# A hybrid decoder layer on one core: the loads and adaLN matmuls of the head in another order

## The chip, the cores and the metric

The kernel runs on one NeuronCore of a Trainium2 chip. The metric is device microseconds of one execution. A profiled execution gives a trace of the engines: PE (TensorE, with its weight loads as PEld), DVE (VectorE), ACT (ScalarE), POOL (GpSimd), and SP, which here only issues DMAs.

## What is computed

One decoder layer (depth 1) over 320 tokens: 256 of a prompt and 64 of eight samples with eight tokens each. Nine conditioning vectors (one for the prompt, eight for the samples) give shifts, scales and gates (adaLN); all tokens share the weights. D is 2048, the FFN is 5632 wide, there are four heads, everything is float32. Cut to what matters here:

```python
mod = silu(c) @ w_ada + b_ada                      # w_ada is 2048 x 12288
sh1, sc1, g1, sh2, sc2, g2 = split(mod, 6)
h = rmsnorm(x, norm1_g) * (1 + sc1) + sh1
q, k, v, og, u, ga, gb, alr = split(h @ w_in)      # 11280 columns
loga = log_sigmoid(alr @ w_a2 + b_a) / 16
o, s_new = gla(q, k, v, loga, s0)                  # gated linear attention
y_a = rmsnorm(o) * silu(og)
y_b = pool(u)                                      # causal averages, then w_pool
x = x + g1 * ((sigmoid(ga) * y_a + sigmoid(gb) * y_b) @ w_o)
h2 = rmsnorm(x, norm2_g) * (1 + sc2) + sh2
x = x + g2 * ((silu(gate(h2)) * up(h2)) @ w_down)  # then a final rmsnorm
```

The outputs are y for both groups, the new attention states and the new pooling buffers.

## The kernel before

Activations are kept transposed: 16 k tiles of 128 channels by 320 tokens. Each is split into a high part and a rest in the fast float32 form (`hilo`, lines 315 and 316: `hh` on ACT, `hl` on DVE), and so is each weight tile (`split`, lines 151 and 152: `whi` on ACT, `wlo` on DVE). A product is three matmuls, `whi`·`hh`, `whi`·`hl` and `wlo`·`hh` (`mm3`, lines 165 to 167). Weights come by `raw_chunk` (line 143) on SP's queue, at most 512 KB a load, into three buffers.

**The head** is the block under `with tc.tile_pool(name="head")`. It makes the modulation of the first norm and the projections of group 0 (a group is a head h with its share of q, k, u, v, og, ga, gb: 2816 columns). Since the first projection needs a k tile of h, which needs two blocks of 128 columns of w_ada's sections 0 (shift) and 1 (scale), the k tiles are taken in four slices, `SLICES = ((0, 2), (2, 4), (4, 8), (8, 16))`. A slice runs seven units over its k tiles: q, k, u with 256 columns (`proj`) and v, og, ga, gb with 512 (`proj2`). Their sums are added up over the slices in SBUF (`evac`, line 369). While one slice is projected, the list `bg` makes the next slice's k tiles: for every two blocks `hada(0, b, nb)`, `hada(1, b, nb)` and `h_unit(b, nb)`, spread evenly behind the seven units.

`ada` (before only) takes two blocks of one section. It loads four tiles of 512 KB (four k tiles by 256 columns); each tile gives four matmuls with the 32-column stationary `scT[:, k]` (silu of the conditioning vectors), one on each of the four column groups of PE, where column group j sums every fourth k (line 225). A copy (line 228), two transposes (`tr`, line 129) and a reduction over the four groups (line 233) follow, then bias, +1 and norm gain (lines 236 to 240). The ring has seven tiles.

`h_unit` makes a k tile: three transposes of x, a copy to `xT` (line 461), which is written to a DRAM scratch `xspill` from POOL's queue (line 463; it is read back in the output projection), a product with the norm factors `rx` (line 462), the modulation `affine` (lines 320 to 322) and `hilo`. `rx` comes from sums of squares on ACT (line 443).

The low-rank gate projection `alr_proj` uses all 16 k tiles; it stands behind unit k of the last slice and ends with the tile `alr` (line 484). Its weights `walr` (16 columns of w_in), the masks and constants are loaded on POOL's queue; the program has them in the last slice, but nothing holds them there.

**After the head** its pool is closed, and pools for group 0's recurrence and for the rest of adaLN open in the same memory (memsets at line 534 on). Group 0's recurrence and pooling steps (`queue`, taken by `pump`) run between the projections of groups 1 to 3. Those groups have 11 units each over all 16 k tiles, and the rest of w_ada is done in `ada_burst`: four k tiles by eight blocks at a time, where column group j has its own two blocks, and the sum over k is made in PSUM (line 284). q, k, v and u have one buffer each, so group 1's q can be written (line 371) only when group 0's steps have read theirs (line 622 last), and the products of a unit have two PSUM buffers (`pmain`). The output projection and the FFN follow.

The order on each engine is made by a list scheduler: it walks a simulated time line and takes, of what is ready, what stands first in the program. `tc.high_priority()` moves instructions ahead of that, and `tc.issue_after(i)` holds a block's instructions behind instruction i of the same engine.

Of the kernel before, what the change touches and what calls it, by code (L numbers as in the profile page):

```python
# [38 lines left out]
SLICES = ((0, 2), (2, 4), (4, 8), (8, 16))  # L39

# [42 lines left out]
def body(tc, A):  # L83
# [130 lines left out]
    def ada(sec, b0, nb=2, pool=None, bufs=2):  # L214

        pool = pool or apool[0]
        blk = sec * KT + b0
        w = nb * P
        ps = misc()
        step = 8 // nb  # L220
        for k0 in range(0, KT, step):
            raw = raw_chunk(wada[:, k0:k0 + step, blk * P:(blk + nb) * P], step, w, pool, "araw", bufs)
            for i in range(step):
                j, r = (k0 + i) % 4, (k0 + i) // 4
                PE.matmul(ps[32 * j:32 * j + 32, 0:w], lhsT=scT[:, k0 + i, :], rhs=raw[:, i, :],
                          start=r == 0, stop=r == 3, tile_position=(0, 32 * j))
        sb = pool.tile([P, w], F32, tag="adasb", name=nm("adasb"))
        S.copy(sb, ps[:, 0:w])
        pt = misc()
        for i in range(nb):  # L230
            tr(pt[:, i * P:(i + 1) * P], sb[:, i * P:(i + 1) * P])
        dst = mod[:, blk:blk + nb, :]
        V.tensor_reduce(dst, pt[:, 0:w].rearrange("p (b j r) -> p b r j", b=nb, j=4)[:, :, 0:9, :],
                        axis=AX.X, op=ALU.add)
        bb = bada[:, blk:blk + nb].unsqueeze(2).broadcast_to([P, nb, 9])
        V.tensor_tensor(dst, dst, bb, op=ALU.add)
        if sec in (1, 4):
            g = N1G if sec == 1 else N2G
            V.tensor_scalar(dst, dst, 1.0, None, op0=ALU.add)
            V.tensor_tensor(dst, dst, g[:, b0:b0 + nb].unsqueeze(2).broadcast_to([P, nb, 9]), op=ALU.mult)  # L240

# [155 lines left out]
    with tc.tile_pool(name="head", bufs=1) as xp:  # L397
        junk = xp.tile([P, D], F32, name="junk")
        crow = junk[0:9, :]
# [3 lines left out]
        G.memset(xn[2][TS:P], 0.0)  # L403
        x2d = A["x_prompt"][0]
        V.memset(scT, 0.0)
        make_identity(nc, ident)
        pt = misc()
        for k in range(KT):
            tr(pt[:, 16 * k:16 * k + 9], crow[:, k * P:(k + 1) * P])
        csig = xp.tile([P, KT, 9], F32, name="csig")  # L410
        crT = pt[:, 0:256].rearrange("p (k r) -> p k r", r=16)[:, :, 0:9]
        S.activation(csig, crT, AF.Sigmoid)
        V.tensor_tensor(scT[:, :, 0:9], crT, csig, op=ALU.mult)
# [4 lines left out]
        nc.sync.dma_start(vr0, A["b_ada"].rearrange("o (r p) -> (o r) p", p=P))  # L418
        vr1 = xp.tile([4 * KT + 4, P], F32, name="vr1")
        for j, n in enumerate(("norm1_g", "norm2_g", "final_norm_g", "pool_scale")):  # L420
            a = A[n] if n == "final_norm_g" else A[n][0]
            nc.sync.dma_start(vr1[16 * j:16 * j + 16, :], a.rearrange("(r p) -> r p", p=P))
        nc.sync.dma_start(vr1[64:68, :], A["gla_norm_g"][0].rearrange("(r p) -> r p", p=P))

        def hada(sec, b, nb):
            ada(sec, b, nb, *head_ring)

        head_ring = [xp, 7]

        pt = misc()  # L430
# [4 lines left out]
        V.tensor_scalar(bada[:, 4 * KT:5 * KT], bada[:, 4 * KT:5 * KT], 1.0, None, op0=ALU.add)  # L435
        hada(0, 0, SLICES[0][1])
        hada(1, 0, SLICES[0][1])

        ssq = xp.tile([P, 3], F32, name="ssq")
        V.memset(ssq, 1.0)  # L440
        for i in range(3):
            n = P if i < 2 else TS
            S.activation(junk[:n], xn[i][:n], AF.Square, accum_out=ssq[:n, i:i + 1])
        S.activation(ssq, ssq, AF.Sqrt, scale=1.0 / D, bias=epst)
        V.reciprocal(ssq, ssq)
        prs = misc()
        dg = xp.tile([P, 3, P], F32, name="dg")
        for i in range(3):
            V.tensor_scalar(dg[:, i], ident, ssq[:, i:i + 1], None, op0=ALU.mult)
            PE.matmul(prs[:, i * P:(i + 1) * P], lhsT=ones, rhs=dg[:, i], start=True, stop=True)  # L450
        rx = xp.tile([P, T], F32, name="rx")
        V.tensor_copy(rx, prs[:, 0:T])

        def h_unit(k0, nk):
            for k in range(k0, k0 + nk):
                pt = misc()
                for i in range(3):
                    tr(pt[:, i * P:(i + 1) * P], xn[i][:, k * P:(k + 1) * P])
                xT = xp.tile([P, T], F32, tag="xT", bufs=2, name=nm("xT"))
                xh = xp.tile([P, T], F32, tag="xh", bufs=2, name=nm("xh"))  # L460
                S.copy(xT, pt[:, 0:T])
                V.tensor_tensor(xh, pt[:, 0:T], rx, op=ALU.mult)
                nc.gpsimd.dma_start(xspill[k], xT)
                affine(xh, 1, 0, k)
                hilo(hh[k], hl[k], xh)
# [23 lines left out]
        new_gates(g0)  # L489
        for si, (k0, k1) in enumerate(SLICES):  # L490
            if si == 0:
                h_unit(0, SLICES[0][1])
            bg = []
            if si + 1 < len(SLICES):
                n0, n1 = SLICES[si + 1]
                st_ = min(2, n1 - n0)
                for b in range(n0, n1, st_):
                    nb = st_
                    bg += [lambda b=b, nb=nb: hada(0, b, nb), lambda b=b, nb=nb: hada(1, b, nb),
                           lambda b=b, nb=nb: h_unit(b, nb)]  # L500
            elif si == len(SLICES) - 1:
                walr = xp.tile([P, KT, 16], F32, name="walr")
                nc.gpsimd.dma_start(walr, win[:, :, OAL:OAL + 16])
                nc.gpsimd.dma_start(msk, A["ci"])
                cum = xp.tile([P, NM0 + NM1 + NMS], F32, name="cum")
                nc.gpsimd.dma_start(cum, A["cf"][:, CFC:CFW])
                nc.gpsimd.dma_start(cst[:, 2 * P:], A["cf"][:, 0:CFC])
            us = units(0)
            us = [u for u in us if u[0] in "qku"] + [u for u in us if u[0] not in "qku" and u[1] == 0]
            done = 0  # L510
            for ui, (kind, i, col) in enumerate(us):
# [5 lines left out]
                if si == len(SLICES) - 1 and ui == 1:  # L517
                    alr_proj(walr, cum)
                want = len(bg) * (ui + 1) // len(us)
                while done < want:  # L520
                    bg[done]()
                    done += 1
# [376 lines left out]
    def pump(n):  # L899
        for _ in range(min(n, len(queue))):  # L900
            queue.pop(0)()

    nc.gpsimd.dma_start(A["o_ps"][0, :, 0:PB - LS, :], A["state_pool"][0, :, LS:PB, :])

    st, E = gla_steps(g0)
    pst, psy = pool_steps(g0)
# [289 lines left out]
```

## Time and profile before

| | |
|---|---|
| median of 3 runs | 1974.52 us (1974.08 to 1975.68) |
| the profiled execution | 1972.61 us, of which the trace spans 1970.7 us |
| PE, DVE, ACT, POOL busy | 1927.2, 1003.3, 822.3, 204.7 us |
| w_ada loads on SP's queue | 64 of 512 KB |
| w_in loads on SP's queue | 173 |
| HBM read / written | 374.23 / 24.67 MB |
| first projection matmul | 38.40 us |

A row of a group of instructions has line, engine, operation, output and inputs, shapes and count, then the busy time in us and the mean duration in ns, then the idle time of the engine ahead of them and what ended most of it. Matmuls overlap in the trace: a projection matmul lasts some 310 ns in its row, but the next one starts well before that ends, so the distance between starts is what it costs. A row of the time line has the start, the length, the engine, the line and the operation; several alike are merged with their count.

### The profile page before, as it was taken

The page shows a single profiled execution, that of the slowest core. Times are in us where ns is not written, and L with a number is a line of the kernel's source. Part 1 is how long each engine was busy: PE and PEld are TensorE (multiplying, and loading weights), DVE is VectorE, ACT ScalarE, POOL GpSimd, SP SyncE. Part 2 cuts the span into 40 slices and gives each one's busy share as a digit, 9 for nine tenths or more (in the row PEclk, how much of TensorE's full clock was granted, in tenths as well). Part 3 has the DMA queues.
Part 4 walks back from the last instruction along what each step waited for, and adds up shares of the span by engine and source line. Part 5 has one row for each costly group of instructions (what it writes and reads, how often), then busy time and mean ns, then how long its engine had stood idle before and what let it go on. Part 6 is the DMA issues. An engine that isn't in the chain of part 4 may idle for free.

```text
span 1970.7 us, 34879 instructions
## 1 busy us (share of the span) xinstructions
PE 1927.2 (98%) x13900; PEld 1811.9 (92%) x13900; DVE 1003.3 (51%) x1894; ACT 822.3 (42%) x1472; POOL 204.7 (10%) x352
## 2 busy tenths in 40 slices
PE   5999999999999999999999999999999999999998
PEld 3778988988899889988989999999999999999998
DVE  2655655655356535665474444444444444444554
ACT  3323553643345433553344333433333434344444
POOL 1002211221122112111130000000000000000000
PEclk9999999999999999999999999999999999999999
DMA  9995558758865787479935554444444444444443
GB/s 339 340 338 181 189 174 292 246 192 312 279 218 168 267 292 261 129 254 326 320 114 194 191 184 142 149 153 144 157 146 152 149 152 150 150 148 149 140 150 107
DMA packets 310206, 400.95 MB, mean 203 GB/s; under 512 B 12898, under 2 KB 273858, under 8 KB 309706
## 3 DMA queue, kind: packets, MB, share of 16 engines
q1 hardware_dynamic: 279914, 291.17, 45.8%
q0 software_dynamic: 30128, 107.55, 14.8%
q8 instruction: 109, 1.79, 0.4%
q14 instruction: 55, 0.44, 0.1%
HBM read 374.23 MB, written 24.67 MB: 202 GB/s over the span
## 4 chain that ended last, share of the span: by engine, by line
PE 82%; DMA 2%; ACT 1%; DVE 1%; issue 0%; POOL 0%; ACTq 0%; DVEq 0%; POOLq 0%
PE ps L167 25%; PE ps L165 25%; PE ps L166 25%; PE pm L284 3%; PE pm L129 1%; DMA araw<-w_ada 1%; PE pm L779 1%; PE pm L758 1%; DMA raw<-w_o 1%; PE pm L723 1%; DMA raw<-w_in 1%; PE pm L712 0%; DVE wlo L152 0%; PE pm L653 0%; ACT whi L151 0%
## 5 line engine op out<-in xcount | busy, mean ns | idle before, releaser
L152 DVE TENSOR_TENSOR wlo<-raw,whi 128x512 fp32r<-128x512 f32 x941 | 648.9, 694 | 773.6 <-ACT whi L151 760.7
L151 ACT CAST whi<-raw 128x512 fp32r<-128x512 f32 x941 | 579.2, 621 | 899.9 <-PE ps L166 802.2
L165 PE MATMUL ps<-hh,whi 128*128 128x320 f32 x1408 | 441.8, 314 | 3.1 <-ACT whi L151 2.1
L167 PE MATMUL ps<-hh,wlo 128*128 128x320 f32 x1408 | 436.0, 312 | 2.0 <-DVE wlo L152 1.9
L166 PE MATMUL ps<-hl,whi 128*128 128x320 f32 x1408 | 436.4, 310 | 0.0
L165 PE MATMUL ps<-h2h,whi 128*128 128x320 f32 x1408 | 434.6, 309 | 0.0
L166 PE MATMUL ps<-h2l,whi 128*128 128x320 f32 x1408 | 434.3, 309 | 0.0
L167 PE MATMUL ps<-h2h,wlo 128*128 128x320 f32 x1408 | 434.2, 309 | 0.0
L165 PEld LDWEIGHTS ps<-hh,whi 128*128 128x128 f32 x1408 | 264.5, 188 | 27.6 <-issue 16.1
L167 PEld LDWEIGHTS ps<-hh,wlo 128*128 128x128 f32 x1408 | 263.7, 188 | 17.5 <-issue 9.5
L166 PEld LDWEIGHTS ps<-hl,whi 128*128 128x128 f32 x1408 | 264.7, 188 | 4.3 <-issue 3.2
L165 PEld LDWEIGHTS ps<-h2h,whi 128*128 128x128 f32 x1408 | 264.5, 188 | 1.2 <-ACT ah L315 1.2
L166 PEld LDWEIGHTS ps<-h2l,whi 128*128 128x128 f32 x1408 | 264.5, 188 | 0.0
L167 PEld LDWEIGHTS ps<-h2h,wlo 128*128 128x128 f32 x1408 | 264.5, 188 | 0.0
L166 PE MATMUL ps<-al,whi 128*128 128x320 f32 (+1 forms) x668 | 206.3, 309 | 0.0
L167 PE MATMUL ps<-ah,wlo 128*128 128x320 f32 (+1 forms) x668 | 205.7, 308 | 0.0
L165 PE MATMUL ps<-ah,whi 128*128 128x320 f32 (+1 forms) x668 | 205.7, 308 | 0.0
L166 PEld LDWEIGHTS ps<-al,whi 128*128 128x128 f32 x668 | 125.2, 187 | 0.1
L167 PEld LDWEIGHTS ps<-ah,wlo 128*128 128x128 f32 x668 | 125.2, 187 | 0.0
L165 PEld LDWEIGHTS ps<-ah,whi 128*128 128x128 f32 x668 | 125.2, 187 | 0.0
L165 PE MATMUL ps<-mh,whi 128*128 128x320 f32 x256 | 80.3, 314 | 3.3 <-ACT whi L151 2.6
L260 POOL DMA_DIRECT2D araw<-w_ada x64 | 45.7, 718 | 355.6 <-PE pm L284 341.0
(316 smaller groups left out, 1698.5 us busy)
## 6 DMA issues: line engine op xcount, KB each, us to landing
raw<-w_gu SPq DMA_DIRECT2D x176, 512.0 KB, 3.4
raw<-w_in SPq DMA_DIRECT2D x173, 512.0 KB, 3.9
araw<-w_ada POOLq DMA_DIRECT2D x64, 1024.0 KB, 8.0
raw<-w_down SPq DMA_DIRECT2D x80, 512.0 KB, 3.4
raw<-w_ada SPq DMA_DIRECT2D x64, 512.0 KB, 6.3
S<-state_gla POOLq DMA_DIRECT2D x16, 1024.0 KB, 8.8
o_gs<-S POOLq DMA_DIRECT2D x16, 1024.0 KB, 6.1
raw<-w_o SPq DMA_DIRECT2D x32, 512.0 KB, 7.3
```

What stands on the lines that cost most here:

```text
L129: PE.transpose(out, in_, ident[:k, :k])
L151: S.copy(hi, raw)
L152: V.tensor_sub(lo, raw, hi.bitcast(F32))
L165: PE.matmul(ps, lhsT=whi, rhs=xhi, start=start, stop=False)
L166: PE.matmul(ps, lhsT=whi, rhs=xlo, start=False, stop=False)
L167: last_mm[:] = [PE.matmul(ps, lhsT=wlo, rhs=xhi, start=False, stop=stop).ins]
L260: nc.gpsimd.dma_start(t[:, r:r + 2], wada[:, k0 + r:k0 + r + 2, col:col + NBA * P])
L284: last_ada[:] = [PE.matmul(ps[32 * j:32 * j + 32, 0:2 * P], lhsT=scT[:, k0 + r, :], rhs=ada_raw[n][:, r, 2 * j * P:(2 * j + 2) * P], start ...
L723: PE.matmul(pt, lhsT=E["kdn"][:, s, d * P:(d + 1) * P], rhs=E["vn"][:, s], start=s == 0, stop=s == 1)
L758: PE.matmul(pt[32 * j:32 * j + 32, :], lhsT=qeP[:, d, 4 * gg + j, :], rhs=E["S0", gg, d][:, j], start=False, stop=d == 0, tile_position=(0 ...
L779: PE.matmul(pt, lhsT=E["kpn"][:, j, d * P:(d + 1) * P], rhs=E["vp"][:, gg], start=True, stop=True)
```

## The change

- **Queues.** On SP: the conditioning vectors in another layout (128 rows of 128 numbers), x, then the eight w_ada tiles of the first slice (four of each section). The vectors b_ada, norm gains, pool scale and attention norm gain go to POOL's queue. `walr`, masks and constants, the copy of the old pooling state, and the spill of the first eight x tiles are issued in `late_loads`, behind unit q of the last slice and behind the spill of k tile 15.
- **x tiles.** `h_pre` (transposes, copy, product with `rx`) stands ahead of the sums that make the modulation; `h_post` (`affine`, `hilo`) behind them. The copies of k tiles 0 to 7 are kept in `merged[1]` and `merged[3]`, which groups 1 and 3 need later. Sums of squares are made in halves.
- **adaLN.** `ada` is replaced by the class `Ada`: two or four blocks of both sections together. A step is one load of each section (512 KB each); column groups 0 and 1 take the shift's halves, 2 and 3 the scale's, with the same `scT[:, k]`, and the sum over k is made in PSUM. A burst is two steps (2 MB, four k tiles by four blocks, or eight by two), with high priority and behind the last projection matmul made so far. Its place is given by `BURST_AT` (behind which unit of the slice), and each burst starts the loads of the next but one. The closing has one copy, one or two transposes and three DVE operations. The ring has nine tiles instead of seven.
- **The next slice's k tiles** are finished right behind the closing of their `Ada`, in pairs.
- `alr_proj` stands behind unit og (the fifth) instead of unit k (the second) of the last slice.

The diff, cut to its core:

```diff
+BURST_AT = ((2, 4), (2, 3, 4, 5), (0, 1, 2, 3, 3, 4, 4, 5))
...
-        nc.sync.dma_start(crow[0:1, :], A["c_prompt"])
-        nc.sync.dma_start(crow[1:9, :], A["c_sample"])
+        make_identity(nc, ident)
+        nc.sync.dma_start(cr1, A["c_sample"].rearrange("b (k p) -> (b k) p", p=P))
+        nc.sync.dma_start(cr0, A["c_prompt"].rearrange("o (k p) -> (o k) p", p=P))
...
-        nc.sync.dma_start(vr0, A["b_ada"].rearrange("o (r p) -> (o r) p", p=P))
+        nc.gpsimd.dma_start(vr0, A["b_ada"].rearrange("o (r p) -> (o r) p", p=P))
...
+            def burst(self, n, near=True):
+                step, w = self.step, self.nb * P // 2
+                if self.at == 0:
+                    self.ps = misc()
+                with ExitStack() as es:
+                    if near:
+                        es.enter_context(tc.high_priority())
+                        es.enter_context(tc.issue_after(last_mm[0]))
+                    for r in range(self.at, self.at + n):
+                        for i in range(step):
+                            k = r * step + i
+                            for j in range(4):
+                                PE.matmul(self.ps[32 * j:32 * j + 32, 0:w], lhsT=scT[:, k, :],
+                                          rhs=self.raws[r][j // 2][:, i, (j % 2) * w:(j % 2 + 1) * w],
+                                          start=k == 0, stop=k == KT - 1, tile_position=(0, 32 * j))
+                self.at += n
+                if self.at * step == KT:
+                    with tc.high_priority():
+                        self.close()
...
+        AR = 9
+        first = Ada(0, SLICES[0][1])
+        first.load(4)
...
+        for k in range(2):
+            h_pre(k)
+        first.burst(4, near=False)
+        for k in range(2):
+            h_post(k)
...
+        def late_loads():
+            with tc.issue_after(spilled[0]):
+                for k, xT in spill:
+                    nc.gpsimd.dma_start(xspill[k], xT)
+                nc.gpsimd.dma_start(walr, win[:, :, OAL:OAL + 16])
+                nc.gpsimd.dma_start(msk, A["ci"])
+                nc.gpsimd.dma_start(cum, A["cf"][:, CFC:CFW])
+                nc.gpsimd.dma_start(cst[:, 2 * P:], A["cf"][:, 0:CFC])
+                nc.gpsimd.dma_start(A["o_ps"][0, :, 0:PB - LS, :], A["state_pool"][0, :, LS:PB, :])
...
+                todo = [Ada(b, nb) for b in range(n0, n1, nb)]
+                per = 2
+                seq = [(t, i) for t in todo for i in range(0, nb * 2, per)]
+                at = BURST_AT[si]
+                todo[0].load(2 * per)
+                for n, (t, i) in enumerate(seq):
+                    bg[at[n]].append(lambda t=t: t.burst(per))
+                    if n + 2 < len(seq):
+                        bg[at[n]].append(lambda t=seq[n + 2][0]: t.load(per))
+                    if i + per == nb * 2:
+                        for k in range(t.b0, t.b0 + nb, 2):
+                            bg[at[n]] += [lambda k=k: (h_pre(k), h_pre(k + 1)), lambda k=k: (h_post(k), h_post(k + 1))]
...
-                if si == len(SLICES) - 1 and ui == 1:
-                    alr_proj(walr, cum)
+                if si == len(SLICES) - 1:
+                    if ui == 0:
+                        late_loads()
+                    if ui == 4:
+                        alr_proj(walr, cum)
```

More of the change, by code (lines that the diff above doesn't have):

```diff
@@ L212, in body @@
     wdn = A["w_down"][0].rearrange("(kt p) n -> p kt n", p=P)
[L214 to L240, printed above, removed]
     NBA = 8
@@ new lines, in body @@
+        AR = 9
+        first = Ada(0, SLICES[0][1])
+        first.load(4)
+        pt = misc()
+        tr(pt[:, 16:16 + P], cr1)
+        tr(pt[:, 0:16], cr0)
+        csig = xp.tile([P, 16 + P], F32, name="csig")
+        S.activation(csig, pt[:, 0:16 + P], AF.Sigmoid)
+        V.tensor_tensor(scT[:, :, 0], pt[:, 0:16], csig[:, 0:16], op=ALU.mult)
+        V.tensor_tensor(scT[:, :, 1:9], pt[:, 16:16 + P].rearrange("p (b k) -> p k b", k=KT),
+                        csig[:, 16:16 + P].rearrange("p (b k) -> p k b", k=KT), op=ALU.mult)
@@ new lines, in body @@
+        junk = xp.tile([P, D // 2], F32, name="junk")
+        for i in range(3):
+            n = P if i < 2 else TS
+            for c in range(2):
+                S.activation(junk[:n], xn[i][:n, c * (D // 2):(c + 1) * (D // 2)], AF.Square,
+                             accum_out=ssq[:n, i, c:c + 1])
+        rst = xp.tile([P, 3], F32, name="rst")
+        V.tensor_tensor(rst, ssq[:, :, 0], ssq[:, :, 1], op=ALU.add)
+        S.activation(rst, rst, AF.Sqrt, scale=1.0 / D, bias=epst)
+        V.reciprocal(rst, rst)
@@ L430, in body @@
+        rx = xp.tile([P, T], F32, name="rx")
+        dg = xp.tile([P, 3, P], F32, name="dg")
+        prs = misc()
+        for i in range(3):
+            V.tensor_scalar(dg[:, i], ident, rst[:, i:i + 1], None, op0=ALU.mult)
+            PE.matmul(prs[:, i * P:(i + 1) * P], lhsT=ones, rhs=dg[:, i], start=True, stop=True)
+        V.tensor_copy(rx, prs[:, 0:T])
         pt = misc()
@@ L445, in body @@
[L445 to L458, printed above, removed]
-                xT = xp.tile([P, T], F32, tag="xT", bufs=2, name=nm("xT"))
[L460 to L465, printed above, removed]
+        for sec in (1, 4):
+            V.tensor_scalar(bada[:, sec * KT:(sec + 1) * KT], bada[:, sec * KT:(sec + 1) * KT], 1.0, None, op0=ALU.add)
@@ new lines, in body, with h_pre @@
+        xhs, spill, spilled = {}, [], []
+        def h_pre(k):
+            pt = misc()
+            for i in range(3):
+                tr(pt[:, i * P:(i + 1) * P], xn[i][:, k * P:(k + 1) * P])
+            if k < 8:
+                xT = merged[1 + 2 * (k // 4)][:, k % 4]
+            else:
+                xT = xp.tile([P, T], F32, tag="xT", bufs=2, name=nm("xT"))
+            xhs[k] = xp.tile([P, T], F32, tag="xh", bufs=2, name=nm("xh"))
+            S.copy(xT, pt[:, 0:T])
+            V.tensor_tensor(xhs[k], pt[:, 0:T], rx, op=ALU.mult)
+            if k < 8:
+                spill.append((k, xT))
+            else:
+                spilled[:] = [nc.gpsimd.dma_start(xspill[k], xT).ins]
@@ L489, in body @@
         new_gates(g0)
+        for k in range(2):
[3 more added lines that the diff above has]
+            h_post(k)
+        us = units(0)
+        us = [u for u in us if u[0] in "qku"] + [u for u in us if u[0] not in "qku" and u[1] == 0]
+        def late_loads():
[7 more added lines that the diff above has]
+                nc.gpsimd.dma_start(A["o_ps"][0, :, 0:PB - LS, :], A["state_pool"][0, :, LS:PB, :])
@@ L490, in body @@
+        walr = xp.tile([P, KT, 16], F32, name="walr")
+        cum = xp.tile([P, NM0 + NM1 + NMS], F32, name="cum")
         for si, (k0, k1) in enumerate(SLICES):
-            if si == 0:
-                h_unit(0, SLICES[0][1])
-            bg = []
+            bg = [[] for _ in us]
             if si + 1 < len(SLICES):
                 n0, n1 = SLICES[si + 1]
[L496 to L507, printed above, removed]
@@ L508, in body @@
-            us = units(0)
-            us = [u for u in us if u[0] in "qku"] + [u for u in us if u[0] not in "qku" and u[1] == 0]
-            done = 0
+                nb = min(4, n1 - n0)
+                todo = [Ada(b, nb) for b in range(n0, n1, nb)]
[10 more added lines that the diff above has]
+                            bg[at[n]] += [lambda k=k: (h_pre(k), h_pre(k + 1)), lambda k=k: (h_post(k), h_post(k + 1))]
```

78 lines of the change are left out of this document (47 added, 31 removed).

## The prediction

> **What bounds the kernel now.** I read the page first, then the busy time by stretches, then the waits of TensorE (PE), and only then the first 40 us in order of time.
>
> ```profile
> span 1970.7 us, 34879 instructions
> ...
> PE 1927.2 (98%) x13900; PEld 1811.9 (92%) x13900; DVE 1003.3 (51%) x1894; ACT 822.3 (42%) x1472; POOL 204.7 (10%) x352
> ```
>
> PE is busy for all but 43.5 us. The stretches (columns: stretch, length, busy us and count of PE, PEld, DVE, ACT, POOL, granted clock, DMA share, GB/s) say where those are:
>
> ```profile
> 10.00:20.00 10.00, 2.85 (x18) 0.79 (x18) 1.72 (x8) 6.62 (x8) 0.00 (x0) 1.00 0.99 288
> 20.00:50.00 30.00, 24.01 (x197) 15.13 (x194) 11.18 (x31) 10.76 (x21) 1.11 (x2) 1.00 1.08 386
> 50.00:80.00 30.00, 30.00 (x241) 23.11 (x240) 18.22 (x48) 10.84 (x23) 2.14 (x4) 1.00 1.02 350
> 90.00:100.00 10.00, 9.94 (x87) 7.13 (x87) 8.28 (x22) 4.03 (x9) 1.07 (x2) 1.00 0.85 272
> 38.40:251.40 213.00, 208.64 (x1580) 178.89 (x1577) 124.38 (x279) 87.70 (x172) 30.03 (x65) 1.00 0.79 268
> ```
>
> From 38.4 us on PE hardly stops; its longest class of waits between there and 251 us is
>
> ```profile
> PE ps L165 <- ACT whi L151: 1.6, 2, 1.3
> ```
>
> (1.6 us in total). So only two things can shorten this kernel: an earlier first projection matmul, or less PE time. A faster transfer in the middle of the head buys nothing by itself; a later one can cost. The start, in order of time:
>
> ```profile
> 2.75 1.32 POOL L503 DMA_DIRECT2D walr<-w_in  x1
> ...
> 10.89 9.13 SPq L143 DMA_DIRECT2D raw<-w_ada  x7
> ...
> 30.75 1.08 PE L225 MATMUL pm<-raw,scT 128*32 128x256 f32 x8 [2.31 <-DMA raw<-w_ada]
> ...
> 33.80 0.18 DVE L240 TENSOR_TENSOR mod<-mod,vec 128x18 f32<-128x18 f32 x1
> ...
> 36.02 0.41 DVE L320 TENSOR_SCALAR xh<-xh,mod 128x256 f32<-128x256 f32 x1
> ...
> 38.40 0.56 PE L165 MATMUL ps<-hh,whi 128*128 128x320 f32 x2
> ```
>
> The last w_ada tile that the first two k tiles need reaches PE at 30.75, the modulation is done at 33.98, the x tiles follow on DVE at 36.02, and the projections begin at 38.40. The first w_ada load is issued at 10.89 only, because SP held it for an x load:
>
> ```profile
> SPq L143 <- DMA xn<-x_prompt: 4.4, 1, 4.4
> ```
>
> That x load was the fourth on the queue and w_ada the twelfth: eight are in flight at most. What the transfers did meanwhile, us by us:
>
> ```profile
> GB/s 0 8 197 262 393 401 434 426 238 156 193 218 154 277 431 283 349 293 316 368 364 373 385 375 379 383 384 381 388 382 388 382 389 383 388 380 399 388 408 414
> ```
>
> Full rate (393 to 434) from 4 to 8 us, then 154 to 277 for six: the tables (walr with its rows of 16 numbers, issued at 2.75, and the others behind it) and the short vectors move in those.
>
> **The change, part by part.**
>
> *Queue order and tables.* SP now has two c loads and three x loads ahead of w_ada, which becomes sixth to thirteenth; walr, masks and constants leave the head's beginning altogether, and eight of the 16 x tiles are spilled after the head's w_ada. I assume the rate then stays at the 386 of the 20 to 50 us row. By the shapes, x is 2.62 MB, c and vectors 0.15 MB, eight w_ada tiles 4.19 MB: 6.96 MB, of which the first 3 us move 0.2. So 3 + 6.76/0.386 = 20.5 us to the last byte. Bounds: 434 throughout gives 18.6; three w_in tiles of 0.26 MB and a ninth w_ada tile ahead of the last one give 24. Landing and the matmuls of the last step (two tiles) are 1.1 us by the 30.75 row, 2.2 at worst: 22.0.
>
> *x tiles made ahead.* rx, the transposes and xh no longer stand between modulation and projection. What stays is 30.75 + 1.08 to 33.98, 2.1 us (one transpose instead of two, three small DVE operations instead of four: 1.9), and 36.02 to 38.40, 2.4 us. First projection at 22.0 + 4.3 = 26.3, bounds 23.9 to 30.5. **Gain 12.1 us**, 8 to 14.5. Squares, rx and x copies must be done by 22 us; before, they waited for x tiles that landed among the tables; x now lands ahead of w_ada, which hides them.
>
> *Bursts of 2 MB on column groups.* A visit of PE to one 512 KB w_ada tile looks like this:
>
> ```profile
> 99.81 0.31 PE L165 MATMUL ps<-hh,whi 128*128 128x320 f32 x1
> ...
> 101.29 0.31 PE L166 MATMUL ps<-hl,whi 128*128 128x320 f32 x1
> 101.53 0.64 PE L225 MATMUL pm<-raw,scT 128*32 128x256 f32 x8
> ...
> 102.35 0.30 PE L165 MATMUL ps<-hh,whi 128*128 128x320 f32 x1
> ```
>
> Projection starts are 0.148 us apart (ten steps from 99.81 to 101.29). From the last one before the visit to the second one after it are 1.06 us instead of 0.296, so one tile costs 0.76. The later adaLN code already runs 16 such matmuls together:
>
> ```profile
> 267.87 1.86 PE pm L284 x32
> ```
>
> 1.86 for the same work as four tiles: 0.465 each, so a visit's overhead is 0.30. There are 42 visits in the head, the first and last being
>
> ```profile
> 42.11 0.64 PE L225 MATMUL pm<-raw,scT 128*32 128x256 f32 x8
> ...
> 164.87 0.64 PE L225 MATMUL pm<-raw,scT 128*32 128x256 f32 x8
> ```
>
> and the groups behind 38.4 us are
>
> ```profile
> L225 PE MATMUL pm<-raw,scT 128*32 128x256 f32 x412 | 33.1, 388 | 0.0
> L129 PE MATMUL pm<-cst,xn 128*128 128x128 f32 x42 | 5.7, 273 | 0.0
> L129 PE MATMUL pm<-cst,adasb 128*128 128x128 f32 x26 | 5.1, 278 | 0.6 <-ACT adasb L228 0.5
> ```
>
> 412 at eight a tile are 51.5 tiles. Now 42 x 0.30 + 51.5 x 0.465 = 36.5 us; after, 14 visits (two of the second pair of blocks, four for each of three sets of four) and 56 tiles (five were done in the old idle start): 4.2 + 26.0 = 30.2. **Gain 6.3.** Transposes of the sums fall from 26 to 7, at 5.7/42 = 0.136 each (the x transposes stay): **gain 2.6**. Sum so far 21.0 us.
>
> *What is given back.* (1) Two of four closings now cover four blocks, so four x tiles are finished at once, between slices 1 and 2 behind one short unit. DVE has, per tile,
>
> ```profile
> L316 DVE TENSOR_TENSOR hl<-xh,hh 128x320 fp32r<-128x320 f32 x15 | 7.1, 492 | 1.4 <-ACT hh L315 1.2
> L462 DVE TENSOR_TENSOR xh<-pm,rx 128x320 f32<-128x320 f32 x14 | 6.5, 487 | 0.5 <-ACT xT L461 0.3
> L320 DVE TENSOR_SCALAR xh<-xh,mod 128x256 f32<-128x256 f32 x14 | 5.7, 409 | 0.1
> L322 DVE TENSOR_TENSOR xh<-xh,mod 128x64 f32<-128x64 f32 x14 | 2.7, 221 | 0.0
> ```
>
> 1.8 us (the 221 ns twice), 7.3 for four, beside the unit's own splits; the unit covers 24 x 0.148 = 3.6. Between 0 and 6 us; I take 3, since two tiles can start the next unit.
> (2) Each burst stands in PE's order until all of its 2 MB is there, and projections queue behind it. The last one is wanted at 26.3 + 480 matmuls x 0.148 + 13 visits (28.1) + 35 transposes (4.8) + 3 = 133 us. Until then 48.1 MB must move (x and vectors, all 33.6 of w_ada, 10.5 of w_in, 1.3 of spilled x): 3 + 47.9/0.386 = 127. I take 1 us, 0 to 26 (rival D).
> (3) The head's pool closes behind the low-rank projection (alr), which moves from behind unit k to behind unit og, and the first group's recurrence cannot begin earlier:
>
> ```profile
> 184.98 0.55 DVE L484 SCALAR_TENSOR_TENSOR alr<-alrh,cst,pm 128x320 fp32r<-128x320 f32 x1 [0.44 <-ACT alrh L483]
> ...
> 218.34 1.55 DVE L369 SCALAR_TENSOR_TENSOR og<-ps,og 128x640 f32<-128x640 f32 x2
> ...
> 226.28 0.48 DVE L557 SCALAR_TENSOR_TENSOR w<-w,cst,w 128x256 fp32r<-128x256 f32 x1
> ...
> 233.47 0.51 PE L562 MATMUL pm<-w,alr 128*128 128x256 f32 x3
> ...
> 246.10 0.29 PE L587 MATMUL pm<-cumr,w 128*128 128x272 f32 x1
> ...
> 251.27 0.34 PE L587 MATMUL pm<-cumr,w 128*128 128x400 f32 x1
> ...
> 259.50 0.41 DVE L622 TENSOR_TENSOR w<-EX,q 128x256 f32<-128x256 f32 x1
> ...
> 268.28 0.70 ACT L371 ACTIVATE q<-ps 128x640 f32<-128x640 f32 x1
> ```
>
> Group 0's q is read last at 259.9, 74.4 us after alr; group 1 writes q at 268.3, so there is slack of 8. The last slice ends right ahead of the 251.27 row, og's unit 33 us ahead of that; alr behind it, with 32 matmuls, is ready 28 us ahead of the slice's end. So q comes free 46 us after the slice's end, where before it was 9. Of that chain 6.7 us (226.76 to 233.47) and 4.6 (between the two L587 groups) were its turn on a full PE and vanish when PE is idle: 35. PE meanwhile has group 1's units q and k in two PSUM buffers, each 96 x 0.148 + 2.1 = 16.3: 33. I take 4 us, 0 to 18 (rival C).
> Free: the x squares in halves (ACT idle then), six vector loads moved to POOL (POOL idle till its first spill), 14 late issues on POOL in the last slice, under the 49 us of units before alr needs POOL; without that cover they cost 14 issues, each at most the 1.32 us of walr's.
>
> Sum: -12.1 - 6.3 - 2.6 + 3 + 1 + 4 = **-13.0 us**. The profiled execution took 1972.6, so 1959.6; the median of the runs shown is 1.9 higher: **1961.5**.
>
> [...]
>
> **Rivals.**
> A, the forecast: 1953 to 1972. Chance 0.58.
> B, nothing given back: the scheduler fills PE at the boundary and the chain shortens. -21 us, 1953.5. For it: PE never starved between 38 and 251 us. Against: bunching. 0.10.
> E, transfers at the 350 of the 50 to 80 us row: last load at 140 us, 7 us of waiting instead of 1: 1967.5. 0.06.
> C, the late alr: group 0's pooling product needs both PSUM buffers and stood right behind group 1's q; if it stands ahead of k, PE has 16 us, not 33, to cover 35: 18 to 19 lost instead of 4: 1976, no measurable change. It eats the gain from 17 us of stall on. 0.13.
> D, slower: bursts wait for data. If transfers after 50 us run at the 272 of the 90 to 100 us row, 29.8 MB take until 160: PE waits 26 us: 1974.5 - 21 + 26 + 3 + 4 = 1986. It turns slower (by over 0.2%) below about 295 GB/s. For it: in-order SP, nine tiles of buffer. Against: that row is PE not asking. 0.13.
>
> **How the numbers follow.** 0.2% (4 us) is about what can be told from no change. A, B and E are faster (0.74), C the same (0.13), D slower (0.13). Range: A, B's end and the unknown start below, C above: 1949 to 1977.
>
> **What would show it.** First projection matmul near 26 us and full rate from 4 us on; w_ada in 14 visits; alr ready about 28 us before the last slice's end; a PE stall of a few us once group 1's first two units are done. Wrong, if the first projection stays above 31 us, or PE waits for w_ada sum to over 10 us, or the gain at 250 us of the old order is there but gone by group 1's third unit.

## The result and the profile after

The changed kernel takes 1978.59 us (median of 11 runs, 1975.70 to 1980.06) against 1974.52 us; the ratio is 1.0023, with a 95% interval of 1.0014 to 1.0032. So it is slower by about 4 us where 13 us less were forecast. Time per engine on its page:

```profile
span 1976.8 us, 35003 instructions
...
PE 1920.8 (97%) x13990; PEld 1821.6 (92%) x13990; DVE 1004.1 (51%) x1865; ACT 816.6 (41%) x1463; POOL 204.9 (10%) x357
```

PE does 6.4 us less work (1927.2 before), in a span that is 6.1 us longer: idle PE has grown from 43.5 to 56.0 us. The start, PE's time line:

```profile
25.83 1.07 PE L425 MATMUL pm<-raw,scT 128*32 128x128 f32 x28 [0.41 <-DMA raw<-w_ada]
...
27.26 0.33 PE L130 MATMUL pm<-cst,adasb 128*128 128x128 f32 x1 [0.16 <-ACT adasb L438]
31.30 0.90 PE L166 MATMUL ps<-hh,whi 128*128 128x320 f32 x2 [3.71 <-ACT hh L286]
```

The projections begin at 31.30, which is 7.1 us earlier than before and 5.0 later than forecast. What the transfers did, us by us:

```profile
GB/s 0 38 81 127 410 402 405 426 424 206 196 156 152 306 350 349 346 349 348 347 348 349 349 346 348 349 351 361 334 348 349 345 350 350 347 345 350 349 356 380
```

The tables are gone from the first 40 us, but four slow us (9 to 12) are still there, and behind them the rate is mostly 346 to 350 instead of the 380 or so of before. By stretches (columns as in the prediction; the seventh value is the granted clock):

```profile
31.00:50.00 19.00, 15.57 (x127) 14.23 (x128) 5.39 (x11) 6.68 (x12) 0.00 (x0) 0.79 1.07 371
50.00:80.00 30.00, 29.04 (x282) 25.65 (x281) 17.63 (x36) 10.68 (x20) 0.00 (x0) 1.00 0.77 259
80.00:110.00 30.00, 26.87 (x225) 22.83 (x227) 17.43 (x40) 9.14 (x19) 0.00 (x0) 0.89 0.89 316
235.00:300.00 65.00, 59.50 (x434) 54.94 (x438) 41.27 (x79) 32.77 (x66) 16.61 (x29) 0.97 0.54 175
```

In three of them PE stands idle and the clock is below 1.00; before, it was 1.00 in all four. The waits of PE from 31 to 300 us (total, times, longest) name four stops:

```profile
PE ps L166 <- ACT hh L286: 6.8, 2, 3.7
PE pm L130 <- DMA S<-state_gla: 4.2, 1, 4.2
PE ps L166 <- ACT whi L152: 3.3, 2, 3.1
PE pm L652 <- ACT w L640: 2.2, 1, 2.2
```

Counted from the traces, the time (us) at which the n-th matmul of the group projections (4224 in all, 1056 in the head) starts:

```
n                      1     132     264     528    1056    4224
before             38.40   66.17   97.20  159.81  251.12  872.46
after              31.30   62.96   93.87  161.51  252.60  877.75
e1 (alr early)     30.38   60.72   91.81  158.43  248.49  868.51
e4 (start alone)   32.15   62.02   93.04  157.15  249.12  871.02
e9 (ring aligned)  29.66   58.59   89.35  155.94  247.32  872.99
e14 (e1 and e9)    29.60   57.80   88.40  154.54  243.06  865.01
e11 (best)         31.35   58.78   89.97  153.72  242.53  863.29
```

Each row is one execution. e4 and e15 are the same kernel, and e15's row reads 33.06, 62.24, 93.27, 158.78, 250.77 and 872.54, up to 1.7 us from e4's; so a difference of 2 us or less between two rows shows little. Of the 7.1 us of head start, 3.3 are left after 264 matmuls; at the end of the head (n = 1056) the kernel is 1.5 us behind, and 3.8 more go in the groups that follow.

Three of the stops are read from the time line. PE around 94 us:

```profile
92.08 0.31 PE L167 MATMUL ps<-hl,whi 128*128 128x320 f32 x1
92.23 0.31 PE L168 MATMUL ps<-hh,wlo 128*128 128x320 f32 x1
...
94.02 0.49 PE L130 MATMUL pm<-cst,xn 128*128 128x128 f32 x3
97.64 0.90 PE L166 MATMUL ps<-hh,whi 128*128 128x320 f32 x2 [3.13 <-ACT hh L286]
...
98.61 0.47 PE L168 MATMUL ps<-hh,wlo 128*128 128x320 f32 x1
98.88 0.47 PE L166 MATMUL ps<-hh,whi 128*128 128x320 f32 x1
```

This is the boundary of slices 1 and 2, where four x tiles are finished at once. Behind the stop matmuls start 0.27 us apart instead of 0.15, for 6.0 us: the granted clock is 0.50 from 97.0 to 103.9 us and 1.00 before and after. The same goes with the stops at 27, 41 and 232 us (3.7, 3.1 and 4.2 us long): the clock is 0.50 from 28.8 to 35.6, from 45.8 to 49.2 and from 237.0 to 240.4 us, and 4.3, 3.4 and 3.4 us of that lie behind the stop (at 41 us the matmuls first start 0.15 us apart again, from 44.18 on). So each costs about 2 us more than its idle time (an estimate: 3.4 to 6.0 us x (1 - 0.147/0.267) = 1.5 to 2.7). A shorter stop went either way: e4 and e15, the same kernel, both stand for 2.10 us at 149 us, and only e15 goes on with the longer matmuls of half clock, 0.47 us instead of 0.31 (its mean clock from 110 to 235 us is 0.99, e4's 1.00; e4 first):

```profile
149.24 0.41 PE L165 MATMUL ps<-hh,whi 128*128 128x320 f32 x1 [2.10 <-ACT whi L151]
149.49 0.31 PE L166 MATMUL ps<-hl,whi 128*128 128x320 f32 x1
```

```profile
149.48 0.48 PE L165 MATMUL ps<-hh,whi 128*128 128x320 f32 x1 [2.10 <-ACT whi L151]
149.75 0.47 PE L166 MATMUL ps<-hl,whi 128*128 128x320 f32 x1
```

From n = 264 to n = 528 e15 takes 1.4 us longer than e4 (65.51 against 64.11).

At 41 us PE waits for a weight tile, and ACT, which makes `whi` of it, waits for the load:

```profile
43.51 1.14 ACT L152 CAST whi<-raw 128x512 fp32r<-128x512 f32 x2 [3.65 <-DMA raw<-w_in]
```

SP's issues (time of the issue, its length):

```profile
32.06 2.83 SPq L144 DMA_DIRECT2D raw<-w_ada  x2
34.98 2.02 SPq L144 DMA_DIRECT2D raw<-w_in  x3
```

The tiles of unit v are issued behind two w_ada tiles for a later burst and come too late.

The stop at 232 us, with the half clock behind it:

```profile
236.66 0.40 PE L130 MATMUL pm<-cst,sp 120*128 120x120 f32 x2 [4.20 <-DMA S<-state_gla]
...
237.77 0.47 PE L168 MATMUL ps<-hh,wlo 128*128 128x320 f32 x1
238.03 0.47 PE L166 MATMUL ps<-hh,whi 128*128 128x320 f32 x1
```

It begins on POOL. POOL's time line after, then before:

```profile
220.14 0.41 POOL L533 MEMSET alr<- 2x384 f32 x1 [4.87 <-DVE alr L531]
...
222.57 1.47 POOL L231 DMA_DIRECT2D araw<-w_ada  x2
224.04 0.57 POOL L884 DMA_DIRECT2D sp<-state_pool  x1
...
225.37 1.52 POOL L812 DMA_DIRECT2D S<-state_gla  x2
```

```profile
185.65 0.41 POOL L486 MEMSET alr<- 2x384 f32 x1 [5.89 <-DVE alr L484]
...
189.78 0.57 POOL L819 DMA_DIRECT2D sp<-state_pool  x1
...
190.45 1.51 POOL L747 DMA_DIRECT2D S<-state_gla  x2
```

The end of alr closes the head's pool, and the states of pooling and attention can only be loaded behind that: 34 us later than before, right ahead of the transposes of `sp` that PE has next in its order. The load of `sp`, behind two loads of w_ada, lands 12.3 us after its issue. PE waits 4.2 us for it, and everything queued behind those transposes waits too.

### The profile page after: what moved, and what is told of

Its sections match the earlier page's. It is cut to its first block, busy times and chain, and to the rows that moved or that the text cites. A ratio compares the mean times of both kernels' runs of the same rounds, so it can differ in the third digit from the quotient of the medians.

```text
span 1976.8 us, 35003 instructions
## 1 busy us (share of the span) xinstructions
PE 1920.8 (97%) x13990; PEld 1821.6 (92%) x13990; DVE 1004.1 (51%) x1865; ACT 816.6 (41%) x1463; POOL 204.9 (10%) x357
## 4 chain that ended last, share of the span: by engine, by line
PE 91%; DMA 4%; DVE 1%; ACT 1%; SPq 1%; issue 0%; POOL 0%; ACTq 0%; POOLq 0%; DVEq 0%
PE ps L166 27%; PE ps L168 27%; PE ps L167 27%; PE pm L255 3%; PE pm L425 1%; PE pm L130 1%; DMA raw<-w_o 1%; SPq L144 1%; DMA araw<-w_ada 1%; PE pm L844 1%; PE pm L823 1%; PE pm L788 1%; DMA S<-state_gla 1%; DMA raw<-w_ada 0%; DMA raw<-w_in 0%
## 5 line engine op out<-in xcount | busy, mean ns | idle before, releaser
L231 POOL DMA_DIRECT2D araw<-w_ada x64 | 45.8, 719 | 342.0 <-PE pm L255 338.1
```

The lines of the kernel that those rows point to most:

```text
L231: nc.gpsimd.dma_start(t[:, r:r + 2], wada[:, k0 + r:k0 + r + 2, col:col + NBA * P])
```

## The experiments

Each ratio is to the kernel before, run beside the experiment on the same chip. The experiments ran in four groups on four chips, so between groups ratios are compared and not times; a difference of two ratios is uncertain by some 0.0012 to 0.0018 (2.4 to 3.6 us).

**e1: alr early.** The alr matmuls go back behind unit k of the last slice, and their tables are loaded behind the spill of k tile 11, still late.

```diff
-                    if ui == 4:
+                    if ui == 1:
                         alr_proj(walr, cum)
...
+                if si == 2 and ui == 3:
+                    tables()
```

> The changed kernel with one move undone: the low-rank projection stands behind unit k of the last slice again, and walr, masks and constants are loaded behind the spill of k tile 11 so that it can. Theory (four stalls of PE, each followed by a stretch at half clock, hand the gain back): the 4.4 us that PE stands at 232 us for the pooling state and the 2.2 us at 273 us go, and with them 2 us of matmuls at half rate: 1970 to 1972 us. Rival (the time went into the bursts' own PE work, or into a later stage by chance of the schedule): no more than 2 us, 1977 to 1979.

Measured: 0.9979 (0.9970 to 0.9987), 1971.33 us. By the ratios the late alr costs 1.0023 - 0.9979 = 0.0044, or 8.7 us; with the ring of w_ada aligned (e9 against e14 below) it is 0.0057, or 11.3. PE's waits from 31 to 300 us now:

```profile
PE ps L166 <- ACT hh L286: 7.4, 2, 4.3
PE ps L166 <- ACT whi L152: 5.0, 4, 2.5
PE ps L168 <- DVE wlo L153: 1.0, 2, 0.8
```

The rows of `S<-state_gla` and L652 are gone; POOL issues these loads early again:

```profile
184.32 0.57 POOL L889 DMA_DIRECT2D sp<-state_pool  x1
...
185.00 1.52 POOL L817 DMA_DIRECT2D S<-state_gla  x2
```

In the count 4.1 us are back at n = 1056 and 5.1 more by 4224. The late alr is shown as the largest cost.

**e4: the start alone.** The kernel before, with small vectors on POOL, identity first and tables held until the spill of k tile 11; its adaLN, its closings and its alr stay.

```diff
-        nc.sync.dma_start(vr0, A["b_ada"].rearrange("o (r p) -> (o r) p", p=P))
+        nc.gpsimd.dma_start(vr0, A["b_ada"].rearrange("o (r p) -> (o r) p", p=P))
...
+                with tc.issue_after(spill11[0]):
+                    nc.gpsimd.dma_start(walr, win[:, :, OAL:OAL + 16])
```

> The kernel before with the queue part of the change alone: vectors on POOL's queue, identity first, walr, masks, constants and the pooling copy held behind the spill of k tile 11. Bursts, x tiles, closing and the place of the low-rank projection as before. Theory (the early start is real, what follows it loses): first projection at 33 to 35 instead of 38.4 us and the time down by as much, 1970 to 1971. Rival (the slow stretch from 8 to 14 us comes from x itself, not from the tables): first projection no earlier than 37 us, 1973 to 1975.

Measured: 0.9982 (0.9973 to 0.9991), 1970.99 us, 3.5 us less than before. First projection at 32.15. Its transfers:

```profile
GB/s 0 8 197 270 377 426 404 438 339 165 174 219 350 386 387 381 387 386 386 381 389 381 385 382 384 385 385 386 385 384 385 369 402 429 411 391 408 384 384 385
```

The slow us are there without tables, but 381 to 389 follow, not 348. So the start is a gain, and something in the rest of the change lowers the rate. Not all of the start arrives at the end: 6.2 us at the first projection are 2.0 at n = 1056 (one trace), and one of the losses is the 2.1 us stop at 149 us, which the kernel before does not have.

**e2: w_in first.** The second half of the next slice's w_ada loads is issued behind unit k instead of at once.

```diff
-                todo[0].load(2 * per)
+                todo[0].load(per if si == 0 else 2 * per)
+                if si == 0:
+                    bg[1].append(lambda t=todo[0]: t.load(per))
```

> The changed kernel with half of the second pair's w_ada loads (four of eight tiles) moved behind unit k of slice 0, so that w_in of the fourth unit stands ahead of them on SP's queue. Theory (stalls and half clock): the 3.0 us stall at 41 us goes, and with it some 2 us of matmuls at half rate: 1973 to 1974 us. Rival (transfers are short there anyway, so a wait for w_ada takes its place): first stall gone, a wait of 2 us or more ahead of the second burst, 1977 to 1979.

Measured: 1.0012 (1.0004 to 1.0021). The stop at 41 us is still 2.4 us: the scheduler issued the same loads at nearly the same time (the w_in tiles of unit v at 34.05 instead of 34.98), since nothing held them. Inconclusive; e6 holds them.

**e3: closing early.** Slice 1 takes its bursts one unit earlier, so that two units instead of one stand behind the closing and its four x tiles.

```diff
-BURST_AT = ((2, 4), (2, 3, 4, 5), (0, 1, 2, 3, 3, 4, 4, 5))
+BURST_AT = ((2, 4), (1, 2, 3, 4), (0, 1, 2, 3, 3, 4, 4, 5))
```

> The changed kernel with the four bursts of slice 1 one unit earlier each, so that two units instead of one cover the closing and the four k tiles behind it. Theory (stalls and half clock): the 3.2 us stall at 94 us goes, and with it 2 us of half clock: 1973 to 1974 us. Rival (bursts wait for their 2 MB): PE waits for w_ada where it now waits for the k tiles, 1977 to 1981.

Measured: 0.9996 (0.9987 to 1.0004). The stop at 94 us goes from 3.1 to about 1. By the ratios that is 0.0027 or 5.3 us; the count has 1.7 us of it at n = 1056 (250.89), and with alr early as well (e5) the ratio moves only from 0.9979 to 0.9975, or 0.8 us. The sign is shown, the size is not: between 1 and 5 us.

**e7: w_ada section by section.** The rate of 348 might come from loads that alternate between two sections of w_ada; here all tiles of one section come ahead of those of the other.

```diff
...
-                    got = []
-                    for sec in range(2):
-                        c0 = (sec * KT + self.b0) * P
...
+                for sec in range(2):
+                    c0 = (sec * KT + self.b0) * P
+                    for r in range(r0, r1):
```

> The changed kernel with one edit: the w_ada tiles of the two sections are loaded one section after the other within a load call, instead of in turns. Theory (taking turns between two sections costs transfer rate: 348 GB/s against the 386 of the kernel before): 380 or more from 14 us on, first projection 1.0 to 1.5 us earlier, and the stall at 41 us shorter by 2 us: 1974 to 1976 us. Rival (the rate is low because nine tiles and x are in flight together): 348 stays, 1978 to 1979 us.

Measured: 1.0022 (1.0012 to 1.0031), and the rate is still 341 to 354 from 15 to 37 us. This theory fell.

**e9: the ring aligned.** Looking at the addresses in the compiled programs gave another: the changed kernel allocates a tile of 24 bytes (`ssq`) ahead of w_ada's ring, which so begins at byte 127200, 224 past a multiple of 256. Before, it began at 134912, a multiple of 256. If that sets the rate, a ring at 127232, the next multiple, brings back the 381 to 389 of e4.

```diff
-        ssq = xp.tile([P, 3, 2], F32, name="ssq")
+        ssq = xp.tile([P, 8, 2], F32, name="ssq")[:, 0:3]
```

> The changed kernel with one edit: the small tile ssq is made 64 bytes long per partition instead of 24, so that the ring of w_ada's tiles behind it begins at byte 127232, a multiple of 256, and no longer at 127200, which is 224 past one (in the kernel before it began at 134912, a multiple of 256). [...] Rival (the rate is set by the queue's order or by memory): it stays at 346-350 GB/s, the first projection at 31.3 us, the ratio at 1.0023.

Measured: 1.0015 (1.0007 to 1.0024); first projection at 29.66. The transfers:

```profile
GB/s 0 47 58 122 413 393 406 417 413 249 211 167 144 354 389 381 389 381 389 381 390 380 390 382 388 380 387 380 369 384 385 385 386 384 386 387 402 414 406 408
```

Forty bytes of padding bring back 380 to 390 GB/s. In the trace that is 1.6 us at the first projection and 5.3 at n = 1056; the ratio moves by only 0.0008, inside both intervals. The traced execution took 1973.32 us, 2.7 less than the median of its runs, so its count says too much; and e1 and e3, with the ring off the boundary, have their first projections at 30.38 and 30.66.

**e16: the kernel before, off the boundary.** The reverse: 224 unused bytes ahead of the ring of before.

```diff
         head_ring = [xp, 7]
+        V.memset(xp.tile([P, 56], F32, name="gap"), 0.0)
```

> The kernel before with one edit: 224 unused bytes per partition ahead of the ring of w_ada's tiles, so that it begins 224 past a multiple of 256, as in the changed kernel. Theory (the address sets the rate): 346-350 GB/s instead of 381-388 wherever w_ada's tiles of 1 KB rows are loaded; the first projection 38.4 to 39.5-40.5 us; ratio 1.0003 to 1.0015. Rival (the rate belongs to the order of the changed kernel): rate, first projection and time as they were, ratio 0.9995 to 1.0005.

Measured: 1.0007 (0.9999 to 1.0016); first projection at 40.70 instead of 38.40.

```profile
GB/s 0 8 180 254 377 393 426 426 221 123 229 176 218 265 413 231 294 284 261 334 355 347 356 348 347 350 349 347 346 351 347 348 345 352 347 347 347 357 338 371
```

From 20 to 37 us the address alone takes the rate to 345 to 356 (364 to 389 before), in a kernel with none of the change's order: that is shown. That it takes time is not shown by this ratio alone, whose interval includes 1. The two rates stand as 386/348 = 1.11; why the address has this effect, no run shows.

**e10: x_sample on POOL's queue.**

```diff
-        nc.sync.dma_start(xn[2][0:TS], A["x_sample"].rearrange("b t d -> (b t) d"))
+        nc.gpsimd.dma_start(xn[2][0:TS], A["x_sample"].rearrange("b t d -> (b t) d"))
```

> The changed kernel with one edit: x_sample (64 partitions, 0.5 MB) is loaded from POOL's queue, ahead of the small vectors, instead of from SP's queue ahead of w_ada. Theory (the 9 to 13 us at 152-206 GB/s are x_sample's own, half of the partitions at half of the rate, and w_ada waits only because it is behind it in the same queue): w_ada runs beside it, the rate stays at 300 GB/s or more from 9 to 13 us, 0.5 to 0.7 MB more have come by 13 us, and the first projection starts 1.5 to 2 us earlier, near 29.5 us; ratio 1.0010 to 1.0016. Rival 1 (the slow stretch has another cause): the stretch stays, first projection 31.3 us, ratio 1.0023. Rival 2 (w_ada takes the rate from x_sample): x_sample lands later, the square sums and transposes behind it too, and the first projection is no earlier though the rate is.

Measured: 1.0017 (1.0009 to 1.0026); first projection at 32.52.

```profile
GB/s 0 36 120 156 352 254 156 239 320 400 398 365 336 351 346 347 348 347 350 347 348 349 348 349 346 349 350 345 359 336 347 349 348 361 379 381 373 351 349 367
```

The slow stretch moves with x_sample, from 9-12 to 5-7 us. So it belongs to that load (64 partitions, 0.5 MB; whether the 64 partitions are the reason, no run tried), but what stands beside it doesn't run at full rate either: by 13 us 3.13 MB have come, 3.02 in the changed kernel. Half of the theory holds, and no time is gained.

**e8: dummy matmuls in the gaps.** 24 matmuls whose result nobody reads: behind the transposes that close the first burst, behind the next slice's first burst (40 us) and behind the x transposes at the boundary of slices 1 and 2.

```diff
+        def fill(after):
+            ps = misc()
+            with tc.high_priority(), tc.issue_after(after):
+                for _ in range(8):
+                    PE.matmul(ps[:, 0:256], lhsT=ones, rhs=scT[:, 0:8, :].rearrange("p k r -> p (k r)"),
+                              start=True, stop=True)
```

> The changed kernel with 24 matmuls added whose result nobody reads, eight in each of three places where PE stands idle: ahead of the first projection, behind the first burst of slice 0, and between slices 1 and 2. Theory (behind each stall the clock is at half for some 4 us): the projections behind these places start 0.147 us apart at once instead of 0.267, the stalls stay, and the time falls by 3 to 6 us, to 1973 to 1976 us, although PE does more work. Rival (the slow starts behind a stall come from weight splits on ACT and DVE that have to catch up): the 0.267 stays and the time is the same or up to 2 us longer, 1978 to 1981 us.

Measured: 1.0013 (1.0004 to 1.0022). By stretches:

```profile
31.00:50.00 19.00, 16.96 (x150) 14.89 (x151) 6.45 (x12) 6.70 (x12) 0.00 (x0) 1.00 1.07 371
80.00:110.00 30.00, 30.00 (x274) 24.95 (x273) 18.60 (x41) 8.93 (x19) 0.00 (x0) 1.00 0.96 339
```

The clock is 1.00 where it was 0.79 and 0.89: that it falls for want of work on PE is shown. What it costs is less sure. The count is 3.3 us ahead at n = 1056 (249.32) and 2.4 at 4224 (875.32), but e7's is 2.9 ahead at n = 1056 (249.67) with no gain in its ratio. By the ratios it is 0.0010 or 2.0 us, with intervals that overlap, and less than I gave it.

**e5, e6, e11, e12: together.** e5 is e1 with e3. e6 adds w_ada section by section, priority for the first two `h_post`, and a hold of the loads that e2 could not move:

```diff
+                    def rest(t=todo[0]):
+                        with tc.issue_after(last_raw[0]):
+                            t.load(per)
+                    bg[3].append(rest)
...
+        with tc.high_priority():
+            for k in range(2):
+                h_post(k)
```

e11 is e6 with the aligned ring; e12 is e11 with the dummy matmuls.

> The changed kernel with two of its moves undone or shifted: the low-rank projection behind unit k with its tables loaded in slice 2, and the bursts of slice 1 one unit earlier. Theory (stalls, each with half clock behind it): the two gains found one by one add up, -7.3 and -3.8 from the changed kernel: 1967 to 1969 us. Rival (one of them only moved a wait to where the other sits): no better than 1971 us.

> As the kernel before it in this list, and in addition: w_ada tiles of a section one after the other instead of in turns, the second half of the second pair's w_ada held on SP's queue behind w_in of unit v, and the first two k tiles finished with priority. Theory (what is left at the head's start is order on the queues): first projection at 28 to 29 us instead of 31, the stall at 41 us under 1 us, together another 4 to 6 us: 1962 to 1965 us. Rival (the early stretch is short of transfer rate, so any order leaves the same wait): stall at 41 us still over 2 us, 1967 to 1969 us.

> The version with five edits (alr matmuls early, closing early, w_ada section by section, second half of the next slice's w_ada held behind w_in, priority for the first x tiles), 1965.5 us so far, with the 64-byte ssq as well. Theory (w_ada's rate counts at the start here too): 381-388 GB/s from 13 us on, 1.3 to 2.5 us less, 1963.0 to 1964.2 us, ratio 0.9946 to 0.9953. Rival (what comes after the burst, the splits and the affine, sets the start and the saving is lost there): 0.9957 to 0.9961.

> The same with the 24 idle-time matmuls on top (8 behind the transposes that close the first burst, 8 behind the next slice's first burst, 8 behind the boundary of slices 1 and 2). Theory (half clock behind each stop costs about 1 us at each of the places that are left): clock 1.00 from 31 to 50 and from 80 to 110 us, 1.5 to 2.5 us less than without them, ratio 0.9935 to 0.9945. Rival (the stops are now short enough, and the fillers only push real work back): no less than without them, 0.9946 to 0.9961.

Measured: e5 0.9975 (0.9966 to 0.9984), e6 0.9959 (0.9947 to 0.9972), e11 0.9948 (0.9936 to 0.9961; 1962.98 us against 1973.10 beside it), e12 0.9949 (0.9937 to 0.9961). e11 is the best version, faster than both kernels. In e6 the wait for `whi` at 41 us is gone. The dummy matmuls do nothing more in e12, although the clock is 1.00 from 31 to 50 us with them, where e11 has 0.91; where the saving goes is not shown.

**e14 and e15: what is left of the change.** e14 is the changed kernel with e1's and e9's edits only; e15 is e4 once more, run beside e14.

> The changed kernel with the two edits that did most by themselves: the alr matmuls and their tables early, and the 64-byte ssq (w_ada's ring on a multiple of 256). What it tells: what is left of the change when its two worst steps are mended, against the start alone (the next kernel of this call, whose ring is on such a multiple too). Theory: the bursts and the closings on PSUM earn the net 4.9 us that the sum gave them (6.3 + 2.6 - 3 - 1): ratio to the kernel before 0.9952 to 0.9960, 4 to 6 us below the start alone. Rival (the stops at 41 and 94 us and the half clock behind them take back most of it): 0.9965 to 0.9980, 0 to 3 us below the start alone.

> The kernel before with the start of the change alone, once more, beside the last one on the same chip. 0.9982 as it was, within its interval of 0.9973 to 0.9991.

Measured: e14 0.9958 (0.9944 to 0.9972; 1964.84 us), e15 0.9981 (0.9973 to 0.9990; 1970.63 us). The difference, 0.0023 or 4.5 us, lies in the range of the theory, though the two intervals nearly touch. e14 by stretches:

```profile
31.00:50.00 19.00, 18.04 (x210) 16.55 (x210) 6.70 (x13) 7.96 (x13) 0.00 (x0) 0.93 0.98 364
80.00:110.00 30.00, 26.86 (x252) 22.35 (x250) 18.16 (x42) 9.52 (x19) 0.00 (x0) 0.94 0.88 327
235.00:300.00 65.00, 63.55 (x482) 58.05 (x481) 40.06 (x78) 31.84 (x64) 7.81 (x12) 1.00 0.62 195
```

From 235 to 300 us PE does 4 us more than in the changed kernel, but the stop at the boundary (80 to 110 us) is as it was. The expectation left out that the start alone (e4, e15) doesn't have the x tiles made ahead, so 2.6 to 3.5 of the 4.5 us may be theirs (first projection at 29.60 against 32.15 and 33.06).

## Why the prediction was wrong

The forecast was 1961.5 us; with the two edits of e14 the changed kernel does come to 1964.84. That this is near the forecast is luck: e14 takes the late alr back, and without its 4 us the sum is -17.0, where e14's ratio gives -8.3. The parts were mostly of the right kind, but the steps were mis-sized, all to one side, and two costs were in none of them: the ring's address and the half clock.

- **Queue order, 12.1 us: failed, 7.1 measured.** The step "I assume the rate then stays at the 386 of the 20 to 50 us row" put the last w_ada tile at about 21 us; its matmuls began at 25.83. Three things are behind it. The prediction gave the slow us of before to the tables; e4 and e10 show that four of them are x_sample's. At the 402 to 426 GB/s ahead of them, taken as 400, the four us from 9 to 13 would have moved 1.6 MB instead of 0.71, which is 2.3 us at 386. The rate behind them is 348, by an address that no trace shows (e9, e16): 1.3 us for the 4.45 MB from 13 to 25.8 us. And some 0.5 MB of other loads came with it (7.4 MB by 25.8 us, 6.96 in the sum), 1.4 us more. The result is outside the bounds of 23.9 to 30.5, since those held the third alone.
- **x tiles made ahead: right.** From the last tile's matmuls to the first projection 5.5 us (25.83 to 31.30) against 1.1 + 4.3.
- **Bursts and closings, a gain of 8.9 less 4 given back: a gain, but its size is not shown.** The scheduler broke up the bursts of the last slice, so that the trace has 21 visits where 14 were forecast. Between n = 1 and 1056, e14 is 3.5 us shorter than e4 (213.46 against 216.97) and 4.3 shorter than e15, where the sum's four terms gave 4.9. By the ratios e14 is 4.5 us below e15 in all, and with the earlier first projection taken off, 1 to 2 us are left. In e14 the clock is 0.93 from 31 to 50 us and 0.94 from 80 to 110, so behind the start the half clock took part of it.
- **Four x tiles at once, 3 us: the stop was right (3.1 us), the half clock behind it was missed** (6.0 us at the slower distance; e8).
- **Bursts that wait for data, 1 us: right, and rival D is wrong.** From 50 to 80 us the transfers run at only 259 GB/s, and yet PE waits for w_ada nowhere from 31 to 300 us. The order on SP made a stop all the same, at 41 us (3.1 us): not a burst that waits for w_ada, but a projection whose w_in stands behind w_ada. The prediction had "in-order SP" in rival D, in the wrong direction.
- **Late alr, 4 us: failed, 8.7 measured** (e1). The step followed one chain, from alr to the buffer of group 1's q, and so did rival C. The pool's end also holds the state loads on POOL, with PE's `sp` transposes behind them (4.2 us, then half clock); the q chain itself showed up as 2.2 us at L652, far from rival C's 18 (which of the two rows takes how much of the 8.7, no run tells).

By the sum, where the 17.1 us between -13.0 and +4.1 went: 5.0 at the first projection; 4.7 on alr; about 2.0 for the half clock; and for the ring's address behind the start 3.6 by e9's trace (5.3 at n = 1056 less 1.6), but next to nothing by e9's ratio, which is 1.6 in all. That leaves some 2 to 5 us, for the stop at 41 us (3.1 us, and 1.6 in e9) and the bursts, which no run measured by themselves. These sizes mix counts of one trace each with ratios and overlap in part (a stop and the clock behind it), so the split is good to a few us only. What the ring's address is worth in time is the least certain: by ratios 1.6 (e9), 2.2 (e6 to e11), 4.1 (e1 to e14) and 1.4 us (e16), all with one sign, and in each pair the intervals overlap or touch.

## What to carry over

When a step moves the close of a pool, list everything that is allocated behind that close, loads on other queues too, and not only the chain that made you look. When a kernel's tiles are re-declared, look at where the buffers of its transfers begin: a tile of 24 bytes ahead of a ring took a tenth of the load rate (348 GB/s instead of 386), and neither the code nor the waits show it. And look at the clock behind a stop of PE: the four of 3.1 to 4.2 us here each cost an estimated 1.5 to 2.7 us more than their idle time. Before a count in one trace is used as a cost, hold it against a second trace of the same kernel: here two were 1.7 us apart.

## What the runs showed of the hardware

- Loads of 1 KB rows into a ring that begins 224 bytes past a multiple of 256 ran at 334-361 GB/s, mostly 345-352 (14 to 37 us in the changed kernel and e7, 14 to 33 in e10, 20 to 37 in e16), the same loads on a multiple at 364-390 (20 to 36 us in the kernel before, 14 to 31 in e4, 14 to 28 in e9). e7 loads section by section and runs at 341-354, so that order made no difference off the multiple. 127200 is no multiple of 128 or 64 either; whether 256 or one of these counts, no run shows. The ring of w_in's tiles begins 128 past a multiple of 256 in all kernels; nothing else was tried there.
- The load of x_sample (64 partitions, 0.5 MB) goes with a rate of 144-254 GB/s for the whole core for three to four us (9 to 13 us in the changed kernel and e9, 9 to 12 in e4), and takes it with it to another queue (5 to 8 us in e10).
- With four stops of PE of 3.1 to 4.2 us between 27 and 241 us of the changed kernel's trace the granted clock was 0.50 for 6.8, 3.4, 6.8 and 3.4 us, begun between 1.2 us after the start of the stop and 1.7 us after its end; meanwhile projection matmuls started 0.267 instead of 0.147 us apart. After 2.10 us this happened in one execution of a kernel (e15) and not in another (e4).
